# One transformer-like layer on one core: block transposes on VectorE, an accumulating residual and fewer loads for the weight sums

## The chip, the cores and the metric

The kernel runs on one core of a Trainium2 chip, in one launch. The metric is the device time of one execution in microseconds (us). The engines are PE (matrix multiply; PEld is its weight load), DVE (VectorE), ACT (ScalarE), POOL (GpSimd) and SP, which here issues nearly all DMAs. Each engine runs its own instructions strictly in the order in which the program put them; between engines, semaphores order them. All arithmetic and all data in DRAM are fp32.

## The reference

One layer over 2048 tokens of width 1024, with 256 memory tokens and a hidden width D_FF of 2816:

```python
u = rms_norm(h, g_mix_pre[l])
z = u @ w_in[l]
ya = swa_with_sinks(...)          # 64-wide heads, chunk-banded window
yh = hgrn2(...)                   # gated linear recurrence, 4 heads of 128
y = jnp.concatenate([ya, yh], axis=-1) @ w_out[l]
h = h + rms_norm(y, g_mix_post[l])
u = rms_norm(h, g_x_pre[l])
m = rms_norm(mem, g_mem[l])
y = cross_attention(u, m, wq_x[l], wk_x[l], wv_x[l], wo_x[l])
h = h + rms_norm(y, g_x_post[l])
u = rms_norm(h, g_ffn_pre[l])
y = (jax.nn.silu(u @ w_gate[l]) * (u @ w_up[l])) @ w_down[l]
h = h + rms_norm(y, g_ffn_post[l])
```

## The kernel before, in words

**How a large product is made.** Every fp32 factor is split into a high part (ACT copies it to the fp32r type, L994) and the rest (DVE subtracts, L997). A product is then three matmul passes: high by high, high by low, low by high (L1138, L1139, L1140 in `products`). On top of that, each block of 256 rows by 1024 columns is made by a Strassen-Winograd scheme of seven products instead of eight (`seven`, L1142). One of the seven is a **step**: four k-tiles by three passes, 12 matmuls of 128x128 stationary by 128x512 moving. The seven stationary operands S of a block are formed as it comes (`streamed`, L1072): two loads "sraw", some sums on DVE (L1113), and the splits. The seven moving operands T of a stage stay in SBUF over many blocks (`resident`, L1001). Three of them are plain quarters of the stage's matrix. The other four are sums of quarters, which are made ahead of the stage by `combined` (L1034): loads of quarters into tiles called "extra" (or "g"), a DVE operation of 128x1024 (L1041), and a store to a DRAM buffer (qk_s, vo_s, u_s, d_s0 to d_s2, out_s), from which `resident` later loads them as "row" (for out_s also as "z").

**The stages**, in order: the projections of w_in (to 200 us), the two mixing branches (to 600 us), the folding of cross-attention's four weight matrices into two (`fold_cross`, to 760 us), and then the list of `jobs` which `phases` (L1226) runs:

- mixed: concatenated branches times w_out, residual, two norms (763 to 930 us)
- scores: queries times the folded keys, softmax (to 1110 us)
- values: probabilities times the folded values, `value_block` (L1617) (to about 1270 us)
- FFN, first and second token half (to about 2080 us)
- three parts of the down projection (to 2536 us)

In the first three and in the down parts a block is two tiles of 128 tokens, n and n+1. There are 8 blocks to a stage, of 7 steps each.

**What sets the order.** `phases` is a Python generator that emits one step of PE work at a time. Between two steps it emits, for each block that has ended, one more piece of its follow-up work (the generators `after`, which "yield" between pieces: one yield is one step of delay), the S tiles that are needed two steps on (`upto(need[g + 2])`), and the loads and splits of the next T. So the place of a piece on DVE, ACT, POOL and SP is counted in steps. `queued` and `behind` hold work back until an instruction that was emitted before is reached.

**A block of values.** `out` brings the two result tiles into SBUF and ACT squares them (tiles "junk", L1513). The follow-up: `rstds` turns four sums of squares into two factors by three small POOL operations (L1524, L1526, L1528); DVE scales both tiles (L1637); the rows of the residual h1, loaded by SP into two more row tiles, are added by DVE (L1641); SP stores the sum to `out`; ACT squares again; `rstds` again; DVE scales again (L1650) and the result is u, the input of the FFN. `transposed` (L1391) turns each tile of u with 8 PE transposes into two PSUM banks (L1399) and two ACT copies (L1400), and SP stores it to `u_d`, which holds features by tokens. For n of 4 to 7, `token_sums` also makes the T sums of the FFN's first half there. The FFN reads T from `u_d`: columns 0 to 1023 for the first token half, the rest for the second.

**What else exists already.** `blocked` and `store_blocked` (L1403, L1410) transpose a tile on DVE in 32x32 blocks (L1407) and store it in four parts; the results of mixed and scores go that way, and `streamed` reads them with `blocked=True`. `add` (L1540) is a DMA from POOL's queue that adds DRAM rows to an SBUF tile; the last down part uses it.

Of the kernel before, what the change touches and what calls it, by code (L numbers as in the profile page):

```python
# [11 lines left out]
F32 = mybir.dt.float32  # L12
# [36 lines left out]
class Layer:  # L49
# [111 lines left out]
    def run(self):  # L161
# [14 lines left out]
        self.u_d = tc.dram_tile([KT, P, T], F32, name="u_d")  # L176
# [17 lines left out]
    def mix(self):  # L194
        tc, I = self.tc, self.I
        kw = dict(reuse_waits="tile")
        with contextlib.ExitStack() as left:
# [66 lines left out]
            with (  # L264
# [20 lines left out]
    def fold_cross(self):  # L285
# [57 lines left out]
        for h in range(4):  # L343
            banks = [[self.bank(k) for k in "sh"] for _ in range(2)]
            for i in range(2):
# [6 lines left out]
                self.split(raw, wh, wl, "A")  # L352
                for mt in range(2):
# [107 lines left out]
    def in_first(self):  # L461
# [84 lines left out]
        phases = self.phases([(lambda i, j, a, n: raw[i, j][:, a:a + n, :], 4, blocks, None, {})], T)  # L546
# [454 lines left out]
    def resident(self, get, nk, key, dst, keep, sums):  # L1001
# [32 lines left out]
    def combined(self, get, nk, dst):  # L1034
# [3 lines left out]
        for a, b in halves:  # L1038
# [4 lines left out]

            for x, y, key in (((0, 1), (0, 0), 5), ((1, 1), (0, 1), 7), (None, (0, 0), 6), (None, (1, 0), 4)):
# [181 lines left out]
    def phases(self, jobs, first, prologue=None):  # L1226
# [51 lines left out]
        def half(g, tile):  # L1278

            if current[0] is None:  # L1280
# [14 lines left out]
                current[:] = [(k, self.resident(fetch(n, tile), jobs[n][1], p, dst, keep[n], jobs[n][3] is not None)), 0]  # L1295
# [54 lines left out]
        for _, nk, bl, _, beside in jobs:  # L1350
# [69 lines left out]
    def w_out(self, t, i, j, k0, n):  # L1420
        for s in range(1 if i else 2):
            d = t if i else t[64 * s:64 * s + 64]
            r = 512 + k0 * P if i else 256 * s + 64 * k0
            p = P if i else 64
            self.load(d, self.I["w_out"][r:r + p * n, j * 512:(j + 1) * 512].rearrange("(k p) d -> p k d", p=p))

    def sums(self, name, src, nk, *tiles):
# [8 lines left out]
        return dst, lambda: self.combined(get, nk, dst)  # L1436
# [13 lines left out]
    def jobs(self):  # L1450
# [7 lines left out]
        def ffn_u(b):  # L1458
            return lambda t, i, j, k0, n: self.load(
                t, self.u_d[4 * i + k0:4 * i + k0 + n, :, b * TB + j * 512:b * TB + (j + 1) * 512]  # L1460
                .rearrange("k p t -> p k t"))
# [4 lines left out]
        def sums(name, src, nk, other=None):  # L1466
            return self.sums(name, src, nk, self.extra_tile, other or self.gain_tile)
# [10 lines left out]
        jobs = [(self.w_out, 4, kinds([self.mixed_block(n) for n in range(0, NT, 2)], 1), self.out_sums, {1: [qk_s[1]]}),  # L1478
# [325 lines left out]
```

## Time and profile before

| | us |
|---|---|
| median of 3 runs | 2538.45 (2537.29 to 2541.59) |
| the profiled execution | 2537.71 |
| its span in the profile | 2536.0 |

The span is what the trace covers; 1.7 us of the execution lie around it. The granted PE clock was 0.998 of full speed over the span. A row of the timeline gives start, duration, engine, line, operation, `out<-in`, the shapes, and in brackets the idle time of that engine just before and what ended it. A matmul of the main products has a duration of 0.39 us, but they overlap: one starts every 0.2275 us. A row of windows gives, for a stretch of time, the busy time and count of each engine, the granted clock, the mean busy share of the 16 DMA engines and their GB/s. Tile names are the program's with the numbers left out; `psm` is the PSUM of the main products, `pss` one for transposes and small products, `psh` one of the fold.

### The profile page before, as it was taken

The numbers are of one execution on the slowest core, as the hardware profiler recorded it, in microseconds if no ns is written. First come the engines' busy times: TensorE is split into PE (matmuls) and PEld (weight loads), VectorE is DVE, ScalarE is ACT, GpSimd is POOL, SyncE is SP. The second block draws the span as 40 slices with busy tenths as digits, with TensorE's granted clock in tenths as the row PEclk, the third lists the DMA queues.
The fourth block names the chain that finished last, engine by engine and source line by source line (L and its number), as shares of the span: only waits on it lengthen the run. The fifth ranks groups of instructions, "written<-read, shape, count | busy, mean of one in ns | idle before, by whom it ended". The sixth has DMA issues, their size and how long they took to land.

```text
span 2536.0 us, 34175 instructions
## 1 busy us (share of the span) xinstructions
PE 2495.5 (98%) x11942; PEld 2085.2 (82%) x11942; DVE 1795.1 (71%) x2863; ACT 1261.0 (50%) x2627; POOL 378.1 (15%) x540
## 2 busy tenths in 40 slices
PE   9999999999999999999999999999999999999998
PEld 8878888888997778878878888888888888888886
DVE  8885588986556889888876655576566557574766
ACT  5553466654565576566753333353333335443543
POOL 4331344321401112112100000000000000000022
PEclk9999999999999999999999999999999999999999
DMA  6455644673897997857954522254465334564776
GB/s 200 149 166 174 179 143 156 211 239 110 265 322 277 311 329 203 272 186 242 338 177 162 170 83 92 75 199 161 155 216 195 137 121 158 179 186 108 232 174 151
DMA packets 314445, 482.13 MB, mean 190 GB/s; under 512 B 22048, under 2 KB 194080, under 8 KB 314272
## 3 DMA queue, kind: packets, MB, share of 16 engines
q1 hardware_dynamic: 308224, 457.92, 54.2%
q0 software_dynamic: 6048, 22.02, 4.9%
q8 instruction: 94, 1.54, 0.2%
q14 instruction: 79, 0.65, 0.1%
HBM read 313.14 MB, written 166.72 MB: 189 GB/s over the span
## 4 chain that ended last, share of the span: by engine, by line
PE 78%; DVE 8%; DMA 7%; issue 3%; ACT 3%; POOL 1%; SPq 1%; DVEq 0%; POOLq 0%; ACTq 0%
PE psm L1140 21%; PE psm L1138 21%; PE psm L1139 21%; PE psg L158 2%; PE psg L157 2%; PE psg L156 2%; DVE T L997 1%; DVE S L997 1%; DMA qd<-z_d 1%; DVE sum L1113 1%; DVE row L1407 1%; DMA h1t_d<-row 0%; DMA y_d<-sg 0%; DMA qk_s<-extra 0%; ACT junk L1513 0%
## 5 line engine op out<-in xcount | busy, mean ns | idle before, releaser
L1138 PE MATMUL psm<-T,S 128*128 128x512 f32 x2680 | 1033.8, 390 | 14.1 <-ACT part L1153 7.8
L1139 PE MATMUL psm<-T,S 128*128 128x512 f32 x2680 | 1042.3, 390 | 1.2 <-DVE T L997 1.1
L1140 PE MATMUL psm<-T,S 128*128 128x512 f32 x2680 | 1029.7, 390 | 4.8 <-DVE S L997 4.8
L1138 PEld LDWEIGHTS psm<-T,S 128*128 128x128 f32 x2680 | 502.9, 188 | 126.9 <-ACT part L1153 12.9
L1140 PEld LDWEIGHTS psm<-T,S 128*128 128x128 f32 x2680 | 503.1, 188 | 111.9 <-DVE S L997 7.8
L1139 PEld LDWEIGHTS psm<-T,S 128*128 128x128 f32 x2680 | 503.2, 188 | 107.3 <-DVE T L997 4.1
L994 ACT ACTIVATE S<-sum 128x512 fp32r<-128x512 f32 (+1 forms) x370 | 223.9, 620 | 372.7 <-PE psm L1140 270.1
L997 DVE TENSOR_TENSOR S<-sraw,S 128x512 fp32r<-128x512 f32 (+1 forms) x315 | 210.9, 678 | 213.9 <-ACT S L994 211.0
L1153 ACT ACTIVATE part<-psm 128x512 f32<-128x512 f32 x285 | 168.7, 597 | 252.9 <-PE psm L1140 235.2
L997 DVE TENSOR_TENSOR S<-sum,S 128x512 fp32r<-128x512 f32 (+1 forms) x388 | 257.4, 673 | 41.8 <-ACT S L994 38.0
L994 ACT ACTIVATE S<-sraw 128x512 fp32r<-128x512 f32 (+1 forms) x300 | 184.5, 618 | 111.2 <-PE psm L1140 107.0
L1546 POOL DMA_DIRECT2D y_d<-row x16 | 14.0, 877 | 1077.0 <-DVE row L1728 1026.1
L997 DVE TENSOR_TENSOR T<-row,T 128x1024 fp32r<-128x1024 f32 (+1 forms) x112 | 130.9, 1183 | 29.1 <-ACT T L994 27.9
L156 PE MATMUL psg<-u,whi 128*128 128x512 f32 x320 | 127.9, 400 | 0.8 <-DVE z L725 0.8
L158 PE MATMUL psg<-u,wlo 128*128 128x512 f32 x320 | 127.4, 399 | 0.0
L157 PE MATMUL psg<-u,whi 128*128 128x512 f32 x320 | 127.2, 398 | 0.0
L1513 ACT ACTIVATE junk<-row 128x512 f32<-128x512 f32 x160 | 99.6, 624 | 48.3 <-DVE row L1535 27.4
L994 ACT ACTIVATE T<-row 128x1024 fp32r<-128x1024 f32 (+1 forms) x112 | 113.4, 1032 | 11.1 <-DMA row<-in_w_down_dram 3.8
L1679 DVE TENSOR_TENSOR row<-psm,part 128x512 f32<-128x512 f32 x66 | 43.7, 687 | 67.7 <-PE psm L1140 67.7
L997 DVE TENSOR_TENSOR wlo<-raw,whi 128x1024 fp32r<-128x1024 f32 x52 | 64.1, 1233 | 34.3 <-ACT whi L994 22.7
L1688 DVE TENSOR_TENSOR part<-psm,part 128x512 f32<-128x512 f32 x66 | 43.8, 687 | 59.8 <-PE psm L1140 59.6
L1728 DVE TENSOR_TENSOR row<-psm,part 128x512 f32<-128x512 f32 x72 | 49.1, 688 | 49.5 <-PE psm L1140 49.4
(354 smaller groups left out, 3557.6 us busy)
## 6 DMA issues: line engine op xcount, KB each, us to landing
sraw<-in_w_gate_dram SPq DMA_DIRECT2D x44, 512.0 KB, 3.7
sraw<-in_w_up_dram SPq DMA_DIRECT2D x44, 512.0 KB, 3.7
hid_d<-row SPq DMA_DIRECT2D x44, 512.0 KB, 2.7
sraw<-hid_d SPq DMA_DIRECT2D x32, 512.0 KB, 4.2
sraw<-in_w_in_dram SPq DMA_DIRECT2D x48, 256.0 KB, 3.8
z_d<-pair SPq DMA_DIRECT2D x20, 512.0 KB, 3.3
raw<-in_w_in_dram SPq DMA_DIRECT2D x20, 512.0 KB, 5.3
z_d<-z SPq DMA_DIRECT2D x20, 512.0 KB, 3.6
```

What stands on the lines that cost most here:

```text
L156: nc.tensor.matmul(ps, ah, bh, start=(i == 0), stop=False)
L157: nc.tensor.matmul(ps, ah, bl, start=False, stop=False)
L158: nc.tensor.matmul(ps, al, bh, start=False, stop=(i == n - 1))
L994: self.nc.scalar.activation(hi, raw, AF.Copy)
L997: self.nc.vector.tensor_tensor(lo, raw, f32(hi), ALU.subtract)
L1138: nc.tensor.matmul(ps, s[:, 0, k, :], t[:, 0, k, :], start=st, stop=False, **kw)
L1139: nc.tensor.matmul(ps, s[:, 0, k, :], t[:, 1, k, :], start=False, stop=False, **kw)
L1140: nc.tensor.matmul(ps, s[:, 1, k, :], t[:, 0, k, :], start=False, stop=sp, **kw)
L1153: nc.scalar.activation(t, ps, AF.Copy)
L1513: self.nc.scalar.activation(junk, a, AF.Square, scale=float(D) ** -0.5, accum_out=to)
L1688: nc.vector.tensor_tensor(c, a, c, ALU.add)
L1728: nc.vector.tensor_tensor(d, a, b, ALU.add)
```

## The change

1. **Values, second token half (n of 8 and more, 8 tiles).** u is not transposed on PE. DVE transposes it in 32x32 blocks, and four stores to a tile put it into a new buffer `ut_d`. T of the FFN's second half (and its sums u_s) is read from `ut_d`, and `resident` splits it with rearranged patterns (`bytoken`). `u_d` keeps the first half alone.
2. **The residual there.** The 8 SP loads of h1 rows and the 8 DVE additions become 8 accumulating DMAs from POOL's queue, issued right behind the first scaling, and one more yield follows.
3. **The sums.** `combined` gets a third tile and loads each quarter once: 4 loads for a half of the k-tiles in place of 6, each issued 4 yields ahead of its use in place of 3. It holds for qk_s, vo_s, u_s and the three d_s; out_s keeps the old way. There are as many DVE operations and stores as before.
4. **w_out** is laid out anew on the host, so that a load of it is one transfer with rows of 4 KB.
5. **`halved`.** The first S tiles of the mixed job are queued behind a split (on ACT) late in the fold.

```diff
+        self.u_d = tc.dram_tile([KT, P, TB], F32, name="u_d")
+        self.ut_d = tc.dram_tile([NPB, 2, P, 512], F32, name="ut_d")
...
                 with self.queued(self.folded):
                     next(phases)
+                with self.queued(self.halved):
+                    next(phases)
+                    next(phases)
...
                 self.split(raw, wh, wl, "A")
+                if j == 3:
+                    self.halved = self.traced(mybir.EngineType.Activation)
...
+            if bytoken:
+                v = t.rearrange("p n (a k c) -> p k (n a) c", **bytoken)
+                c = v.shape[-1]
+                self.split2(v, *(dst[:, e, :, a * P:b * P].rearrange("p k (m c) -> p k m c", c=c) for e in range(2)),
+                            "A")
+                return
...
+            if three:
+                x = get(0, 0, 1, a, b - a)
+                t = get(1, 1, 1, a, b - a)
+                for _ in range(4):
+                    yield
+                put(7, t, x, ALU.subtract)
+                o = get(2, 0, 0, a, b - a)
+                for _ in range(4):
+                    yield
+                put(5, x, o, ALU.subtract)
+                yield
+                put(6, o, t, ALU.add)
+                x = get(0, 1, 0, a, b - a)
+                for _ in range(5):
+                    yield
+                put(4, x, o, ALU.subtract)
+                for _ in range(2):
+                    yield
+                continue
...
     def w_out(self, t, i, j, k0, n):
-        for s in range(1 if i else 2):
-            d = t if i else t[64 * s:64 * s + 64]
-            r = 512 + k0 * P if i else 256 * s + 64 * k0
-            p = P if i else 64
-            self.load(d, self.I["w_out"][r:r + p * n, j * 512:(j + 1) * 512].rearrange("(k p) d -> p k d", p=p))
+        self.load(t, self.I["w_out"][i, j, k0 // n])
...
         def ffn_u(b):
+            if b:
+                return lambda t, i, j, n0, n: self.load(
+                    t, self.ut_d[4 * j + n0:4 * j + n0 + n, i].rearrange("n p c -> p n c"))
...
         def sums(name, src, nk, other=None):
-            return self.sums(name, src, nk, self.extra_tile, other or self.gain_tile)
+            return self.sums(name, src, nk, self.extra_tile, other or self.gain_tile, self.row_tile)
...
-            x = [self.rows_of(self.h1_d, n + i) for i in range(2)]
+            late = n < NPB
+            x = [self.rows_of(self.h1_d, n + i) for i in range(2 * late)]
             for i in range(2):
                 nc.vector.scalar_tensor_tensor(y[i], y[i], r[:, i:i + 1], self.g_x_post, ALU.mult, ALU.mult)
-            yield
-            yield
+                if not late:
+                    self.add(y[i], self.h1_d, n + i)
+            for _ in range(2 if late else 3):
+                yield
             for i in range(2):
-                nc.vector.tensor_tensor(y[i], y[i], x[i], ALU.add)
+                if late:
+                    nc.vector.tensor_tensor(y[i], y[i], x[i], ALU.add)
...
             for i in range(2):
+                if n >= NPB:
+                    self.store_blocked(self.ut_d[n - NPB + i], self.blocked(y[i], self.row_tile()))
+                    yield
+                    continue
                 u[i] = self.transposed(y[i], y[i])
                 self.store_transposed(self.u_d, n + i, u[i])
```

How it moves instructions is shown at three places. **PE, in the second half of values**, where tile n = 8 (row_12345 before) is transposed between two steps. Before:

```order
L1140 MATMUL psm_12842<-T_11470,S_12792 128x512
L1399 MATMUL pss_12758<-ident,row_12345 128x128 x4
L1399 MATMUL pss_12764<-ident,row_12345 128x128 x4
L1138 MATMUL psm_12673<-T_11317,S_12690 128x512
L1139 MATMUL psm_12673<-T_11317,S_12690 128x512
```

After (L1169 to L1171 are the same three passes under new line numbers):

```order
L1170 MATMUL psm_12789<-T_11441,S_12742 128x512
L1171 MATMUL psm_12789<-T_11441,S_12742 128x512
L1169 MATMUL psm_12634<-T_11288,S_12651 128x512
L1170 MATMUL psm_12634<-T_11288,S_12651 128x512
```

The eight transposes are gone and one step follows the other directly. It is so for all eight tiles.

**POOL, from the first norm of block n = 8 on** (its sums of squares are q_s_12344 before and q_s_12315 after). Before, the first norm of n = 8, its second norm (q_s_12482), and the first norm of n = 10 (q_s_12564), one after the other:

```order
L1528 TENSOR_TENSOR q_r_12480<-q_w_12478,mhalf 128x2
L1524 TENSOR_TENSOR q_v_12663<-q_s_12482 128x2
L1526 TENSOR_SCALAR q_w_12665<-q_v_12663 128x2
L1528 TENSOR_TENSOR q_r_12667<-q_w_12665,mhalf 128x2
L1524 TENSOR_TENSOR q_v_12696<-q_s_12564 128x2
L1526 TENSOR_SCALAR q_w_12698<-q_v_12696 128x2
L1528 TENSOR_TENSOR q_r_12700<-q_w_12698,mhalf 128x2
```

After (the second norm of n = 8 is q_s_12453, the first of n = 10 is q_s_12531; h_d in the two DMA rows stands for the buffer h1):

```order
L1558 TENSOR_TENSOR q_r_12451<-q_w_12449,mhalf 128x2
L1572 DMA row_12316<-h_d 128x1024
L1572 DMA row_12352<-h_d 128x1024
L1554 TENSOR_TENSOR q_v_12656<-q_s_12453 128x2
L1554 TENSOR_TENSOR q_v_12662<-q_s_12531 128x2
L1556 TENSOR_SCALAR q_w_12658<-q_v_12656 128x2
L1556 TENSOR_SCALAR q_w_12664<-q_v_12662 128x2
L1558 TENSOR_TENSOR q_r_12660<-q_w_12658,mhalf 128x2
L1558 TENSOR_TENSOR q_r_12666<-q_w_12664,mhalf 128x2
```

The two accumulating DMAs stand in POOL's queue, and the second norm of one block and the first norm of the next are interleaved, with the second norm's first operation ahead.

**DVE, at the end of the fold**, where the low parts of the mixed job's first S tiles stand. Before (`kv`, L317, is the low part of the memory's projected values, written in eight pieces, of which the row here is the last; `wlo` is the low part of a weight block of the fold, and the fold's matmuls wait for both):

```order
L997 TENSOR_TENSOR S_8321<-sraw_8317,S_8321 128x512
L997 TENSOR_TENSOR S_8324<-sraw_8317,S_8324 128x512
L997 TENSOR_TENSOR wlo_8162<-raw_8159,whi_8161 128x1024
L997 TENSOR_TENSOR S_8327<-sraw_8319,S_8327 128x512
L317 TENSOR_TENSOR kv_1055_7829<-psh_8080,kv_1055_7828 128x256
L997 TENSOR_TENSOR S_8330<-sraw_8319,S_8330 128x512
```

After:

```order
L1003 TENSOR_TENSOR wlo_8151<-raw_8148,whi_8150 128x1024
L321 TENSOR_TENSOR kv_1055_7818<-psh_8069,kv_1055_7817 128x256
L1003 TENSOR_TENSOR wlo_8169<-raw_8166,whi_8168 128x1024
L1003 TENSOR_TENSOR S_8310<-sraw_8306,S_8310 128x512
L1003 TENSOR_TENSOR S_8313<-sraw_8306,S_8313 128x512
L1003 TENSOR_TENSOR S_8316<-sraw_8308,S_8316 128x512
L1003 TENSOR_TENSOR S_8319<-sraw_8308,S_8319 128x512
```

The S rows, of which three stood ahead of the last kv row, now all stand behind it.

More of the change, by code (lines that the diff above doesn't have):

```diff
@@ L1294, in half @@
                 left[k] = 2
-                current[:] = [(k, self.resident(fetch(n, tile), jobs[n][1], p, dst, keep[n], jobs[n][3] is not None)), 0]
+                current[:] = [(k, self.resident(fetch(n, tile), jobs[n][1], p, dst, keep[n], jobs[n][3] is not None,
+                                                jobs[n][5])), 0]
             k, f = current[0]
@@ L1349, in phases @@
         fresh = False
-        for _, nk, bl, _, beside in jobs:
+        for _, nk, bl, _, beside, _ in jobs:
             for i, (kind, _, out, follow, addend) in enumerate(bl):
@@ L1477, in jobs @@
         d_s = [sums(f"d_s{c}", src, nk) for c, (src, _, nk) in enumerate(down)]
[L1478 to L1480 removed]
+        jobs = [(self.w_out, 4, kinds([self.mixed_block(n) for n in range(0, NT, 2)], 1), self.out_sums, {1: [qk_s[1]]}, None),
+                (qk, 4, kinds([self.score_block(n) for n in range(0, NT, 2)]), qk_s[0], {1: [vo_s[1]]}, None),
+                (vo, 4, kinds([self.value_block(n) for n in range(0, NT, 2)]), vo_s[0], {}, None)]
         for b in range(NB):
```

21 lines of the change are left out of this document (10 added, 11 removed).

## The prediction

> **What bounds the kernel now.** First the page's head, the chain of waits and the list of PE's waits, then the windows by stage.
>
> ```profile
> span 2536.0 us, 34175 instructions
> PE 2495.5 (98%) x11942; PEld 2085.2 (82%) x11942; DVE 1795.1 (71%) x2863; ACT 1261.0 (50%) x2627; POOL 378.1 (15%) x540
> PE 78%; DVE 8%; DMA 7%; issue 3%; ACT 3%; POOL 1%; SPq 1%; DVEq 0%; POOLq 0%; ACTq 0%
> PE psm L1138 <- ACT part L1153: 7.8, 10, 1.4
> PE psm L1140 <- DVE S L997: 4.8, 5, 1.6
> 800.00:930.00 130.00, 125.18 (x546) 101.77 (x545) 112.84 (x148) 80.17 (x186) 26.41 (x46) 1.00 0.96 317
> 1110.00:1310.00 200.00, 194.06 (x906) 158.32 (x906) 165.99 (x209) 128.78 (x275) 32.08 (x48) 1.00 0.75 254
> 1700.00:2080.00 380.00, 380.00 (x1678) 314.75 (x1677) 237.08 (x349) 139.58 (x243) 0.00 (x0) 1.00 0.45 157
> ```
>
> PE is busy for 98% of the span and 78% of the chain that ended last is PE's. Its waits are short, and the two longest entries sum to 12.6 us. The FFN's second half is PE alone: 380.00 us busy of 380, so nothing that only speeds loads or DVE can gain there. 1678 matmuls in 380 us make 0.2265 us for one, and a block of seven steps of 12 takes 84 x 0.2265 = 19.0 us. Two stages touched by the change have idle PE time, mixed (800 to 930, 4.8 us) and values with the switch to the FFN (1110 to 1310, 5.9 us). In both DVE is busy for over 80% (112.84 of 130, 165.99 of 200). So PE work that is taken away counts in full, provided that DVE, in whose queue S and T are made, doesn't end last in its place.
>
> **The PE transposes of the second half.** Removed are 64 transposes and 16 ACT copies.
>
> ```profile
> 1143.94 0.39 PE L1138 MATMUL psm<-T,S 128*128 128x512 f32 x1
> 1144.17 1.03 PE L1399 MATMUL pss<-ident,row 128*128 128x128 f32 x8
> 1144.96 0.47 PE L1139 MATMUL psm<-T,S 128*128 128x512 f32 x1
> 1145.28 0.39 PE L1140 MATMUL psm<-T,S 128*128 128x512 f32 x1
> 1249.79 0.87 PE pss L1399 x8
> L1399 PE MATMUL pss<-ident,row x128: 270/272/273, 1144.2 to 1301.3; 128*128 128x128 f32 x128
> L1400 ACT ACTIVATE row<-pss x32: 576/592/642, 1144.8 to 1301.7; 128x512 f32<-128x512 f32 x32
> ```
>
> Eight transposes of a tile start at 1144.17 and the next product at 1144.96: 0.79 us. The matmul behind that one starts 0.32 later in place of 0.23, which adds 0.09. So a tile holds PE up for 0.88 us, and the chain shows 0.87 for a tile of the second half. Eight tiles: 8 x 0.87 = **-7.0 us**, on the bounding engine, where PE is busy before and behind. ACT loses 16 x 0.592 = 9.5 us, off the chain.
>
> **What DVE gets for it.** Two block transposes to a tile are added, and the residual's addition goes.
>
> ```profile
> L1407 DVE STREAM_TRANSPOSE row<-row x64: 660/672/708, 804.9 to 1106.0; 128x512 f32<-128x512 f32 x64
> L1641 DVE TENSOR_TENSOR row<-row,row x16: 1210/1218/1221, 1122.7 to 1277.8; 128x1024 f32<-128x1024 f32 x16
> ```
>
> 16 x 0.672 = 10.8 us come and 8 x 1.218 = 9.7 go: +1.0 us over some 75 us, beside PE, taken as 0. If DVE has no room there, it is +1.0. [...]
>
> T of the FFN's second half is split with rearranged patterns. The nearest rows are S from plain rows in mixed and from blocked rows in scores:
>
> ```profile
> L994 ACT ACTIVATE S<-sraw 128x512 fp32r<-128x512 f32 x16 | 9.9, 625 | 4.7 <-PE psm L1140 4.7
> L994 ACT ACTIVATE S<-sraw 128x512 fp32r<-128x512 f32 x20 | 12.5, 624 | 8.0 <-PE psm L1140 8.0
> ```
>
> 625 against 624 ns: no price for the pattern. The loads and the 32 stores to `ut_d` carry the same bytes as before. Taken 0.
>
> **The switch from values to the FFN.** PE waits there for a T:
>
> ```profile
> 1283.92 0.50 PE L1139 MATMUL psm<-T,S 128*128 128x512 f32 x1 [0.35 <-DVE T L997]
> 1286.62 0.50 PE L1139 MATMUL psm<-T,S 128*128 128x512 f32 x1 [0.76 <-DVE T L997]
> ```
>
> T's low part is a subtraction behind ACT's copy. ACT gets lighter, but its squares of the last block now wait for an accumulating DMA. The bounds are -1.1 (both waits go) and +2.2 (as long again for each of two). Taken 0.
>
> **`halved`.** At the end of the fold PE waited for DVE:
>
> ```profile
> 743.34 0.68 DVE L997 TENSOR_TENSOR S<-sraw,S 128x512 fp32r<-128x512 f32 x1
> 743.95 0.42 DVE L317 TENSOR_TENSOR kv<-psh,kv 128x256 fp32r<-128x256 f32 x1
> 744.42 0.50 PE L358 MATMUL psh<-whi,kv 128*128 128x512 f32 x1 [0.82 <-DVE kv L317]
> 763.20 0.39 PE L1138 MATMUL psm<-T,S 128*128 128x512 f32 x1
> ```
>
> The kv row starts when the S row ahead of it ends, and PE waited 0.82 us for it. The S rows now stand behind kv: **-0.8 us**, bounds -0.8 and 0. They are late by a few operations of 0.7 to 1.2 us, but the product that reads them starts only at 763.20, almost 19 us on. That row also shows no wait for w_out's loads, so these count 0; the same bytes come in fewer transfers.
>
> **The sums from four loads.** DVE stops twice in mixed for them or near them:
>
> ```profile
> 812.24 1.22 DVE L1041 TENSOR_TENSOR extra<-extra,row 128x1024 f32<-128x1024 f32 x1 [1.99 <-DMA h1t_d<-row]
> 811.32 0.50 PE L1138 MATMUL psm<-T,S 128*128 128x512 f32 x1 [1.72 <-ACT S L994]
> 812.94 0.50 PE L1138 MATMUL psm<-T,S 128*128 128x512 f32 x1 [0.88 <-ACT part L1153]
> 870.36 1.23 DVE L1041 TENSOR_TENSOR extra<-extra,row 128x1024 f32<-128x1024 f32 x1 [1.03 <-DMA qk_s<-extra]
> 873.44 0.50 PE L1140 MATMUL psm<-T,S 128*128 128x512 f32 x1 [1.09 <-DVE S L997]
> ```
>
> The transfers have a mean share of 0.96 in this stage, so a load less is worth something. The bounds are 0 and -(1.72 + 0.88 + 1.09) = -3.7. The first two PE waits begin before DVE's operation at 812.24 and are for ACT, so they need not go. The third follows the DVE stop at 870.36 and has its size. Taken **-1.0 us**. The sums of the down parts lie in the FFN, where PE has no idle time to give back.
>
> **The accumulating residual.** It is a transfer that DVE started from POOL's queue, in place of a load that was issued early and an addition.
>
> ```profile
> L1542 POOL DMA_DIRECT2D row<-y_d x12: 875/882/1237, 2394.5 to 2493.9; - x12
> DMA to landing us min/median/max: 5.0/7.9/8.8
> L75 SPq DMA_DIRECT2D row<-h_d x18: 332/587/1183, 1100.6 to 2479.4; - x18
> DMA to landing us min/median/max: 2.6/5.8/10.6
> L1637 DVE SCALAR_TENSOR_TENSOR row<-row,q_r,g 128x1024 f32<-128x1024 f32 x16 | 19.8, 1281 | 2.0 <-POOL q_r L1528 2.0
> L1524 POOL TENSOR_TENSOR q_v<-q_s 128x2 f32<-128x2 f32 x15 | 7.7, 510 | 135.2 <-ACT junk L1513 135.2
> L1526 POOL TENSOR_SCALAR q_w<-q_v 128x2 f32<-128x2 f32 x15 | 7.7, 512 | 1.3
> L1528 POOL TENSOR_TENSOR q_r<-q_w,mhalf 128x2 f32<-128x2 f32 x16 | 16.3, 1021 | 1.3
> 1210.00:1230.00 20.00, 20.00 (x98) 16.78 (x97) 18.08 (x26) 13.12 (x31) 3.85 (x6) 1.00 1.06 342
> 2440.00:2460.00 20.00, 20.00 (x90) 16.57 (x89) 12.26 (x17) 9.36 (x20) 4.75 (x7) 1.00 0.75 158
> ```
>
> It makes a ring. On POOL the second norm of block n now starts ahead of the first norm of block n+2. That second norm waits for ACT's squares, these for the accumulated tile. And behind the first norm of n+2 DVE's scaling waits, with the S and T splits of the coming steps queued behind it on DVE; PE waits for those. One turn: two scalings 2 x 1.28 = 2.6, the second tile's issue 0.9, landing 7.9, its two squares 1.2 (about what two halves of a copy take, 0.62 each), and six POOL operations 4 x 0.51 + 2 x 1.02 = 4.1: 16.7 us against a block's 19.0. So 2.3 us are left, and landing may take 10.2 us. Each us above that comes three times, at the three blocks that follow another one of the second half. With 7.9 it costs 0. With 10.6, the slowest of SP's loads of such rows, 0.4 x 3 = 1.2. With twice 7.9, 5.6 x 3 = 16.8. The 12 rows of such DMAs come from a stage with DVE busy 12.26 of 20 and transfers at 0.75; in values it is 18.08 and 1.06. So I go near the 10.6 and take **+0.8 us**, bounds 0 and +16.8.
>
> **The reordering elsewhere** (the window branch near 440 to 600, fold, mixed) carries the same work; taken 0, bounds -3 and +3.
>
> **Sum.** -7.0 - 0.8 - 1.0 + 0.8 = -8.0. Against the profiled execution: 2536.0 - 8.0 = 2528.0 for the span, with 1.7 around it 2529.7. That execution lies 0.74 below the median of the runs, so the forecast is **2530.5 us**. Its own range, with 0 to -3.7 for the sums, 0 to 1.2 for the ring and 2 us for the reordering, is 2526 to 2534.
>
> **The rivals.** What counts as no change is 0.2%, 5.1 us.
>
> *A, the ring binds a little* (0.13). Landing takes half as long again as 7.9, 11.9 us: (11.9 - 10.2) x 3 = +5.1 in place of the 0.8, 2534.8, within 0.2%. For it: the 1.06 of transfers. Against it: the longest of twelve took 8.8.
>
> *B, the ring binds in full: slower* (0.14). Landing 15.8 us, or an issue on POOL that is held up as long: 16.8 - 0.8 = 16 above the forecast, 2546.5. The whole gain is gone from a landing of 10.2 + 8/3 = 12.9 us. For it: DVE is idle for only 2 of 20 us there, and SP's stores of the sum, which wait for the accumulate, stand ahead of loads of the next T. Against it: issues took 0.875 to 1.237 us beside a DVE that was busy 61%. [...] The twelve rows here show no issue held for longer than 0.4 us.
>
> *C, DVE becomes the bound in values* (0.09). DVE has 34 us of 200 idle, but in pieces; if S is made late by what PE saves, the first term is lost, +7.0 and +1.0 for DVE's own: 2538.5, no change. Against it: the longest waits of PE for DVE are 4.8 us in the whole run.
>
> *D, the waits go too* (0.08). -7.0 - 0.8 - 3.7 - 1.1 = -12.6: 2525.9.
>
> **How the numbers follow.** Forecast 0.56 and D 0.08 make faster 0.64; A and C make same 0.22; B is slower 0.14. The range 2524 to 2541 leaves out B and a little of D.
>
> **What would show it.** No PE transposes behind about 1210 us, and PE's busy time less by 6.4 to 7. The ring shows in ACT's squares waiting for the accumulating DMA, in its landing time against 10.2 us, and in DVE's scaling waiting for POOL. The sums show in PE's wait near 873, `halved` in that near 744, and the switch in the T waits near 1284. I am wrong if the landing is above 13 us, if PE's idle time between 1110 and 1310 grows by over 3 us, or if a stage that the edits don't touch moves by more than that.

## The result and the profile after

The change makes the kernel slower by 0.2%, which is about what the prediction counted as no change, but clear of the noise. Its median is 2543.64 us over 22 runs, against 2538.82 for the kernel before over 22 runs on the same chips; the ratio is 1.0020, with an interval of 1.0014 to 1.0025. One run of the change (9990.83 us) and one each of x2, x5 and x9 were slow ones, and all ratios leave them out. The prediction was 2530.5 us, faster.

The page of the changed kernel, its first lines and the chain:

```profile
span 2541.5 us, 34022 instructions
PE 2492.7 (98%) x11878; PEld 2081.6 (82%) x11878; DVE 1796.5 (71%) x2871; ACT 1252.9 (49%) x2611; POOL 377.7 (15%) x548
PE 80%; DVE 7%; DMA 5%; issue 3%; ACT 3%; POOL 1%; SPq 1%; DVEq 0%; POOLq 0%; ACTq 0%
```

The 64 transposes are gone from PE (11878 matmuls in place of 11942), yet its busy time falls by 2.8 us and not by 7. Where the time goes is read from the first and last start of lines that both kernels have. First the scalings of values and the first operation on a down block before, then the same two (L1668, L1766) after:

```profile
L1637 DVE SCALAR_TENSOR_TENSOR row<-row,q_r,g x16: 1275/1280/1287, 1120.3 to 1268.6; 128x1024 f32<-128x1024 f32 x16
L1728 DVE TENSOR_TENSOR row<-psm,part x72: 679/691/692, 2116.3 to 2523.6; 128x512 f32<-128x512 f32 x72
```

```profile
L1668 DVE SCALAR_TENSOR_TENSOR row<-row,q_r,g x16: 1277/1282/1286, 1113.3 to 1273.5; 128x1024 f32<-128x1024 f32 x16
L1766 DVE TENSOR_TENSOR row<-psm,part x72: 680/691/692, 2119.5 to 2528.7; 128x512 f32<-128x512 f32 x72
```

At the first scaling the changed kernel is 7.0 us ahead, at the last 4.9 us behind. So in these two traces values, where 7 us were to be gained, lose 11.9; one trace each places such a loss only to a few us. Some of it returns at the switch to the FFN (3.2 us behind at the down parts' start), and another 1.9 us go in the down parts, which no edit touches beyond their sums. The windows of the stage after the change:

```profile
1110.00:1310.00 200.00, 185.05 (x811) 149.89 (x811) 158.75 (x206) 117.89 (x254) 37.06 (x56) 0.97 0.82 250
1210.00:1230.00 20.00, 16.54 (x67) 13.18 (x66) 11.44 (x15) 8.33 (x20) 5.26 (x8) 0.91 0.96 319
1250.00:1270.00 20.00, 15.23 (x60) 12.11 (x59) 16.62 (x20) 12.96 (x25) 4.40 (x8) 0.85 1.01 313
```

PE is idle for 15.0 us in place of 5.9, and the granted clock is 0.97 in place of 1.00 over 200 us, which is an estimated 6 us more (0.03 of 200). The three longest waits of PE in the second half:

```profile
1218.94 0.50 PE L1171 MATMUL psm<-T,S 128*128 128x512 f32 x1 [3.46 <-DVE S L1003]
1265.95 0.79 PE L1169 MATMUL psm<-T,S 128*128 128x512 f32 x1 [4.77 <-ACT part L1184]
1287.66 0.62 PE L1169 MATMUL psm<-T,S 128*128 128x512 f32 x1 [1.93 <-ACT T L1000]
```

Behind the first stands DVE's queue, where the token sums (L1469) wait for the store of u of n = 7; behind the second ACT's queue, where the squares wait for the accumulating DMA:

```profile
1217.59 0.69 DVE L1469 TENSOR_TENSOR row<-row 128x512 f32<-128x512 f32 x1 [5.47 <-DMA u_d<-row]
```

```profile
1259.73 0.63 ACT L1543 ACTIVATE junk<-row 128x512 f32<-128x512 f32 x1 [3.34 <-DMA row<-h_d]
```

The store of u of n = 7 is late because SP issues it late. ACT's copies for it end at 1204.89, but on SP a store of the sum, which waits 2.5 us for the accumulating DMA, and two more issues stand ahead of it (these rows have start, duration, queue and DMA). It is issued 5.9 us after the copies and lands after 6.8. Before, it was issued as soon as the copies had ended, at 1211.77, and landed after 6.0. First the change, then before:

```profile
1207.97 0.38 SPq L78 DMA_DIRECT2D out_dram<-row  x1
1210.80 0.89 SPq L78 DMA_DIRECT2D u_d<-row  x1
```

```profile
1211.79 0.36 SPq L78 DMA_DIRECT2D u_d<-row  x1
```

So both long stalls lead back to a queue that stands at the landing of an accumulating DMA. The DMAs themselves landed as forecast; this is the line of the eight new ones:

```profile
DMA to landing us min/median/max: 5.4/8.5/10.1
```

### The profile page after: what moved, and what is told of

The parts are those of the page before. It is cut to its first block, busy times and chain, and to the rows that moved or that the text cites. A ratio compares the mean times of both kernels' runs of the same rounds, so it can differ in the third digit from the quotient of the medians.

```text
span 2541.5 us, 34022 instructions
## 1 busy us (share of the span) xinstructions
PE 2492.7 (98%) x11878; PEld 2081.6 (82%) x11878; DVE 1796.5 (71%) x2871; ACT 1252.9 (49%) x2611; POOL 377.7 (15%) x548
## 4 chain that ended last, share of the span: by engine, by line
PE 80%; DVE 7%; DMA 5%; issue 3%; ACT 3%; POOL 1%; SPq 1%; DVEq 0%; POOLq 0%; ACTq 0%
PE psm L1171 21%; PE psm L1169 21%; PE psm L1170 21%; PE psg L156 2%; PE psg L157 2%; PE psg L158 2%; DVE S L1003 1%; DVE T L1003 1%; DMA row<-h_d 1%; DMA pair<-in_x_dram 1%; ACT junk L1543 1%; DMA row<-u_s 1%; DMA ut_d<-row 1%; DVE sum L1144 1%; PE psh L157 0%
## 5 line engine op out<-in xcount | busy, mean ns | idle before, releaser
L1169 PE MATMUL psm<-T,S 128*128 128x512 f32 x2680 | 1036.3, 391 | 21.3 <-ACT part L1184 10.4
L1171 PE MATMUL psm<-T,S 128*128 128x512 f32 x2680 | 1032.4, 391 | 7.6 <-DVE S L1003 7.6
L1169 PEld LDWEIGHTS psm<-T,S 128*128 128x128 f32 x2680 | 504.6, 188 | 134.4 <-ACT part L1184 14.8
L1171 PEld LDWEIGHTS psm<-T,S 128*128 128x128 f32 x2680 | 504.9, 188 | 116.3 <-DVE S L1003 11.4
L1000 ACT ACTIVATE T<-row 128x1024 fp32r<-128x1024 f32 (+1 forms) x112 | 113.3, 1029 | 11.8 <-DMA row<-d_s 4.8
L1766 DVE TENSOR_TENSOR row<-psm,part 128x512 f32<-128x512 f32 x72 | 49.2, 688 | 49.4 <-PE psm L1171 49.3
L832 ACT ACTIVATE S<-S,w_mn 128x256 f32<-128x256 f32 (+1 forms) x128 | 63.1, 496 | 42.5 <-DVE w_mn L828 42.0
```

The lines of the kernel that those rows point to most:

```text
L832: nc.scalar.activation(s[:, r, o:], s[:, r, o:], AF.Exp, bias=mn[:, i:i + 1], scale=-1.0, accum_out=den[:, i:i + 1])
L1000: self.nc.scalar.activation(hi, raw, AF.Copy)
L1169: nc.tensor.matmul(ps, s[:, 0, k, :], t[:, 0, k, :], start=st, stop=False, **kw)
L1171: nc.tensor.matmul(ps, s[:, 1, k, :], t[:, 0, k, :], start=False, stop=sp, **kw)
L1766: nc.vector.tensor_tensor(d, a, b, ALU.add)
```

## The experiments

Each kernel is compared with the kernel before on the same chip. The table gives the ratio to it; one thousandth is 2.5 us.

| kernel | ratio, interval |
|---|---|
| the change | 1.0020 (1.0014 to 1.0025) |
| x1 the change, residual loaded | 0.9995 (0.9985 to 1.0005) |
| x2 before, residual accumulated | 1.0016 (1.0004 to 1.0028) |
| x3 the change, sums of six loads | 1.0031 (1.0022 to 1.0041) |
| x4 before, w_out repacked | 0.9988 (0.9978 to 0.9998) |
| x5 the change without halved | 1.0016 (1.0007 to 1.0024) |
| x7 x1, block stores from POOL | 1.0009 (0.9999 to 1.0018) |
| x8 before with sums, w_out, halved | 0.9987 (0.9978 to 0.9996) |
| x9 before, block transposes | 1.0016 (1.0006 to 1.0026) |
| x10 x1, residual added by POOL | 1.0033 (1.0020 to 1.0045) |
| x11 before, 16 more DVE transposes | 1.0019 (1.0008 to 1.0029) |
| x12 before, 32 more stores | 0.9995 (0.9986 to 1.0004) |
| x13 x2, waits later | 1.0018 (1.0009 to 1.0028) |
| x14 x2, sum stored by POOL | 1.0042 (1.0029 to 1.0056) |
| x15 x1 without the additions | 0.9979 (0.9970 to 0.9988) |
| x16 before with sums, w_out | 0.9979 (0.9969 to 0.9989) |
| x17 before, 8 more accumulating DMAs | 1.0018 (1.0009 to 1.0027) |
| x18 before, 8 more plain DMAs from POOL | 1.0005 (0.9996 to 1.0014) |

### Which part costs

x1 undoes the second part, x2 and x4 do one part alone, x3 undoes the third.

```diff
 x1, in value_block of the change
-            x = [self.rows_of(self.h1_d, n + i) for i in range(2 * late)]
+            x = [self.rows_of(self.h1_d, n + i) for i in range(2)]
-                if not late:
-                    self.add(y[i], self.h1_d, n + i)
...
+                nc.vector.tensor_tensor(y[i], y[i], x[i], ALU.add)
```

> The change with its second part undone: the residual rows of the second token half are again loaded by SP and added by DVE, and the third yield goes. Theory R (the accumulating DMA is what costs): in the profile of the change SP's stores of the sum wait for it, and ACT's squares wait for it (3.3 us once), and two of PE's stalls, 3.46 and 4.77 us, follow. Without it both stalls go with the low clock behind them: about 2530 us (2527 to 2533), PE idle time between 1110 and 1310 us under 7 us. Rival T (the block transposes on DVE, or the four stores and the T loads from the new buffer, are what costs): 2541 to 2545 us, stalls of PE of 3 us and more remain.

```diff
 x2, in value_block of the kernel before: the same lines the other way round
+                if not late:
+                    self.add(y[i], self.h1_d, n + i)
```

> The kernel before with the second part alone: the residual of the second half by accumulating DMA from POOL's queue, PE transposes kept. Theory R: slower than before by 8 to 17 us, 2547 to 2555 us, with PE stalls of 3 us and more behind 1195 us. Rival T: within 3 us of before, 2536 to 2541 us.

```diff
 x3, in jobs of the change
-            return self.sums(name, src, nk, self.extra_tile, other or self.gain_tile, self.row_tile)
+            return self.sums(name, src, nk, self.extra_tile, other or self.gain_tile)
```

> The change without its third part: each half of the sums takes six loads again. As the prediction has it the four loads give 1.0 us: 2544.6 us. Rival: the row tile that they hold for longer takes room from the follow-up work, and without it the time is 2 us shorter or more, 2541.5 us or less.

```diff
 x4, in w_out of the kernel before, with the host's repacking
+        self.load(t, self.I["w_out"][i, j, k0 // n])
```

> The kernel before with the fourth part alone: w_out in one load of 4 KB rows. In the trace of the change PE reaches the end of the mixing branches 4.3 us earlier than before, and nothing but this part lies there (22 loads less in SP's queue between 440 and 725 us). Theory W (the loads, by the order that they change): 2534 to 2536 us, PE at the end of the branches 2 to 4.3 us earlier. Rival: the 4.3 us are not this part's, time 2537.5 to 2540 us as the prediction had it at 0.

x2 is 1.6 thousandths slower than before (2544.1 us, between the times of its two theories), and x1 is 2.5 faster than the change: the accumulating residual costs 4 to 6 us against loads and additions on DVE. But x1 only comes back to the kernel before (2538.3 us), where theory R had 2530, so there is a second loss. x3 puts the sums at 1.1 thousandths within the change, about 2.8 us, where 1.0 us was forecast; the intervals of the two ratios overlap. x4 is faster by 1.2 thousandths, near theory W's time. But the 4.3 us that W read from two traces do not bear it out. The first wait in mixed, a gap of 1.72 us for ACT's S, ends at 811.32 in the profile of before and at 806.66 in that of x14, with the same instructions up to there. So one trace against another can't place a gain of 4 us in that part, and where w_out's 3 us arise is left open.

x5 and x9 go on with single parts, x8 leaves the first two out, and x7 tries the first explanation for the second loss.

```diff
 x5, at the start of mixed in the change
-                with self.queued(self.halved):
-                    next(phases)
-                    next(phases)
 x7, in store_blocked, for the eight tiles of values, on top of x1
+            if pool:
+                self.nc.gpsimd.dma_start(dst[:, :, a * P:(a + 1) * P].rearrange("h (b i) s -> i (h b) s", b=4),
+                                         t[a * 32:(a + 1) * 32, :].rearrange("i (g s) -> i g s", g=8))
+                continue
 x8: the kernel before with the diffs of combined, sums, w_out and halved
 x9: the kernel before with the diffs of resident, ffn_u and transposition
+                if n >= NPB:
+                    self.store_blocked(self.ut_d[n - NPB + i], self.blocked(y[i], self.row_tile()))
```

> The change without its fifth part (the first S tiles of mixed are not queued behind the fold's split). As the prediction has it: 0.8 us slower than the change, 2543.5 to 2545 us, and PE's wait for kv near 740 us back. Rival: the late S tiles cost more at the start of mixed than the wait was worth, and the time is 1 us or more below the change.

> The change with the residual loaded again (as in x1_residual_loaded, 2538.3 us) and the 32 stores of the block-transposed tiles issued from POOL's queue in place of SP's. Theory S: in x1's trace the four stores of a tile hold SP's queue for 2.3 to 2.8 us in place of 0.4 for the one store before, the loads of T's sums behind them come late, ACT waits for one 2.54 us, a copy of a result behind it is late, PE stands for 2.71 us and its clock is halved for 10 us behind that. With the stores off SP's queue these go: 2530 to 2534 us, clock not halved between 1190 and 1310 us. Rival D: the loads are late for the transfers' sake, or DVE is what is short, and the time stays at 2537 to 2540 us.

> The kernel before with the third, fourth and fifth part (sums, w_out, halved), PE transposes and loaded residuals kept. If the parts add up as the runs so far have them (w_out alone -3.0, sums -4.0 within the change, halved -0.8 by the prediction): 2531 us. Rival: the sums' gain in the change was one of its own stalls that moved, and here they give 1 us: 2534 us or more.

> The kernel before with the block transposes alone (first part; residual loaded, six loads, old w_out, no halved). Theory S: the 7 us of PE transposes are given back by stalls at the end of values and the halved clock behind them: 2540 to 2547 us, no faster than before. Rival: the first part is worth its 7 us alone and only clashes with another part: 2530 to 2533 us.

x9 finds the second loss: the block transposes alone, with the additions still on DVE, make the kernel before 1.6 thousandths slower, 4 us, though they take 7 us of work from PE. x8 is faster by 1.3 (2535.9 us, as its rival had it, where the sum of the parts was 2531). x5 can't be told from the change (intervals 1.0007 to 1.0024 and 1.0014 to 1.0025), so `halved` did not give 0.8 us that show. x7 refutes theory S, which had 2530 to 2534 us: with the stores off SP's queue it takes 2540.9, and PE still stalls for 2.79 us up to 1269.43. In its trace that wait is for DVE.

### Why the block transposes cost

The view that answers it is the windows of 10 us at the end of values. Before (1260 to 1280), then x1 (1250 to 1270):

```profile
1260.00:1270.00 10.00, 10.00 (x49) 8.36 (x49) 10.00 (x11) 9.85 (x18) 2.38 (x3) 1.00 1.02 384
1270.00:1280.00 10.00, 10.00 (x48) 8.07 (x47) 10.00 (x12) 4.59 (x8) 0.00 (x0) 1.00 0.97 341
```

```profile
1250.00:1260.00 10.00, 9.33 (x41) 7.42 (x40) 10.00 (x14) 8.51 (x18) 4.08 (x6) 1.00 1.00 320
1260.00:1270.00 10.00, 6.46 (x21) 4.42 (x20) 10.00 (x12) 4.88 (x7) 0.00 (x0) 0.81 1.02 361
```

Already before, DVE (the third engine of a row, behind PE and PEld) is busy without a break from 1260 to 1280 us: the follow-up of the last blocks and the low parts of the FFN's T fall together there. PE transposed two tiles meanwhile, at 1266.17 and 1271.39. With block transposes DVE gets 1.34 us more for each tile (2 x 0.672), and PE, which now has less to do, waits. Four kernels test this:

```diff
 x10, on top of x1
-                nc.vector.tensor_tensor(y[i], y[i], x[i], ALU.add)
+                (nc.vector if n < NPB else nc.gpsimd).tensor_tensor(y[i], y[i], x[i], ALU.add)
 x11, in the kernel before
+                if n >= NPB:
+                    self.blocked(y[i], self.row_tile())
 x12, in the kernel before
+                if n >= NPB:
+                    self.store_blocked(self.ut_d[n - NPB + i], y[i])
 x15, on top of x1
-                nc.vector.tensor_tensor(y[i], y[i], x[i], ALU.add)
+                if n < NPB:
+                    nc.vector.tensor_tensor(y[i], y[i], x[i], ALU.add)
```

> x1_residual_loaded (2538.3 us), but the eight additions of the residual run on POOL in place of DVE. Theory D: in x1 DVE is busy for 10.00 of 10 us in 1250 to 1260 and in 1260 to 1270 us, and PE for 6.46 in the second; DVE has become the bound at the end of values, where it also makes the low parts of the FFN's T. Taking 9.7 us from DVE, some 5 of them in that stretch, gives back 4 to 8 us with the halved clock: 2530 to 2534.5 us. Rival S (SP's queue and the transfers of T's sums): DVE idles for what it saves, time 2537 to 2540 us.

> The kernel before with 16 block transposes more on DVE in the second half of values, whose result is stored nowhere; PE transposes and all transfers stay. Theory D: DVE has no room at the end of values (10.00 of 10 us in 1260 to 1280 us before), 16 x 0.67 = 10.8 us of work cost 3 to 8 us: 2541 to 2546 us. Rival S: hidden, 2537 to 2540 us.

> The kernel before with 32 stores more from SP's queue in the second half of values (each tile of u a second time, in four stores of 32 rows, to a buffer that nothing reads). Theory D: 2537 to 2540 us, the queue has room. Rival S: SP's queue is held some 2.5 us a tile and T's loads come late, 2541 us or more.

> x1_residual_loaded (2538.3 us) without the eight additions of the residual of the second token half, which are left out of the computation; the loads stay. Nothing is put on another engine for it. Theory D: DVE is 9.7 us lighter, about 5 of them at the end of values, PE's stalls there shrink and the clock stays whole: 2530 to 2534.5 us. Rival: DVE is full there because its work comes late (loads of T's sums), not because it is too much: 2536.5 to 2540 us.

x11 and x12 separate the theories: 10.8 us of DVE work that nobody reads cost 1.9 thousandths, 4.8 us, and 32 further stores cost nothing that shows. x15 is the other side: 9.7 us less on DVE bring x1's 0.9995 to 0.9979, 2532.7 us. The windows of x11 and of x15:

```profile
1270.00:1280.00 10.00, 8.28 (x39) 5.90 (x38) 9.99 (x12) 9.33 (x13) 0.63 (x1) 1.00 0.84 278
1280.00:1290.00 10.00, 9.64 (x47) 7.74 (x46) 10.00 (x14) 4.71 (x8) 0.00 (x0) 1.00 0.98 334
```

```profile
1250.00:1260.00 10.00, 10.00 (x46) 8.28 (x45) 10.00 (x13) 8.08 (x15) 4.39 (x5) 1.00 1.03 310
1260.00:1270.00 10.00, 8.63 (x37) 6.53 (x36) 9.10 (x11) 5.72 (x8) 1.36 (x2) 1.00 1.01 388
```

In x11 PE keeps its transposes and still loses 1.7 us in 1270 to 1280 with DVE full; over 1110 to 1310 it is idle for 8.9 us, against 5.9 before. In x15 PE is busy for 8.63 of the 10 us in which x1 had 6.46. x10 missed: an addition takes POOL 2.77 to 4.46 us in place of DVE's 1.22, the second norm comes later by that, and DVE stays full until 1290 us. It says nothing for or against DVE as the bound.

x15 comes near the forecast, but not by the forecast's way. It has all parts of the change but the accumulating DMA, whose rows are loaded as before, and DVE carries what the prediction gave it there, 10.8 us more and 9.7 less. x8 has the same other parts and PE's transposes. Between 1110 and 1310 us DVE is busy for 163.4 us in both, yet x15 is only 0.8 thousandths faster (0.9979 against 0.9987), 2 us with room for nothing to some 5, where 7.0 were forecast. DVE is busy for 38.2 of the 40 us from 1250 to 1290 in x15. So the time that PE spent on transposes was in large part time in which DVE would have kept it waiting. x16 below, with PE's transposes kept, is as fast as x15.

### Why the accumulating residual costs

x13 lets three more steps pass before anything waits for the DMA; x14 issues the store of the sum from POOL.

```diff
 x13, on top of x2
-            for _ in range(2 if late else 3):
+            for _ in range(2 if late else 6):
 x14, on top of x2
-                self.store((self.out if n < NT - 2 else self.h2_d)[(n + i) * P:(n + i + 1) * P, :], y[i])
+                (nc.sync if late else nc.gpsimd).dma_start(
+                    (self.out if n < NT - 2 else self.h2_d)[(n + i) * P:(n + i + 1) * P, :], y[i])
```

> x2_residual_added_alone (2544.1 us against 2539.0 of before) with three more yields between the accumulating DMA and what waits for it (SP's store of the sum and ACT's squares). Theory Q (what costs in x2 is that SP's and ACT's queues stand at these two waits): the waits are over when they are reached, 2534 to 2539.5 us. Rival B (the transfer itself, or its issue on POOL, disturbs): 2542 us or more.

> x2_residual_added_alone (2544.1 us against 2539.0 of before) with the stores of the sum, which wait for the accumulating DMA, issued from POOL's queue for the second half. Theory Q2: in x2 SP's store of the sum of n = 8 waits for that DMA, the store of u of n = 7 stands behind it (1215.96 in place of 1211.79 us), DVE's token sums wait 4.73 us for that one, PE stands for 2.80 us and its clock is halved for 6.8 us. With the stores off SP's queue the wait of the token sums falls back to about 1 us and the stall goes: 2536 to 2540.5 us. Rival B (landing, issue on POOL, or the squares' wait): 2542 us or more.

x13 stays slow (1.0018). In its trace no square of ACT waits for the DMA any more between 1190 and 1300 us, and the cost stays, so ACT's wait is not needed for it. But the first store of the sum still stands ahead of the store of u of n = 7, so x13 says nothing of SP's queue. x14 takes the store of the sum off SP, and DVE's token sums still wait for the store of u, even longer than in x2 (4.73 us):

```profile
1220.72 0.69 DVE L1441 TENSOR_TENSOR row<-row 128x512 f32<-128x512 f32 x1 [6.26 <-DMA u_d<-row]
```

As a whole x14 is slower still (1.0042); its traced run is the fastest of its five, 2540.8 us against 2547 to 2550. The store of u can be late in SP's queue, behind ACT's copies, or by its landing. It stood in the queue for 4.8 us in x2 and 3.9 in x14, where before it stood 0.0, and it landed after 7.2 and 9.7, where before it took 6.0. So in x2 it is mostly the queue, and x14, where a store of T's sums and a load stand ahead of it without the store of the sum, does not clear the queue. The landing is the other part. The DMA rows for 1195 to 1295 us show what bears on it. Each row of a queue gives packets, MB and the share of the 16 engines' time; an issue row ends with the median time to landing. Before, then x2:

```profile
q1 hardware_dynamic: 25675, 31.15, 89.8%
u_d<-row SPq DMA_DIRECT2D x8, 512.0 KB, 6.5
```

```profile
q1 hardware_dynamic: 24354, 26.84, 77.1%
q0 software_dynamic: 1152, 4.19, 23.0%
u_d<-row SPq DMA_DIRECT2D x8, 512.0 KB, 8.6
```

The eight accumulating transfers (q0) hold all 16 engines for 23 of 100 us. At the rate of the other queue (31.15 MB in 89.8%) their 4.19 MB would take an estimated 12.1. The two queues together fill 100% of the stretch, and the eight stores of u land 2 us later in the median. The last two kernels take this by itself:

```diff
 x17 and x18, in the kernel before, behind the addition; the result is read by nothing
+                if n >= NPB:
+                    self.add(x[i], self.h1_d, n + i)                                      (x17)
+                    nc.gpsimd.dma_start(x[i], self.h1_d[(n + i) * P:(n + i + 1) * P, :])  (x18)
```

> The kernel before, with eight accumulating DMAs more from POOL's queue in the second half of values, into the residual tiles after they have been added; nothing reads the result, so nothing waits for it but the tiles' next use. Theory X (the accumulating transfer itself: in x2 between 1195 and 1295 us its 4.19 MB took 23.0% of the 16 DMA engines' time, 23.0 us, where at the 31.15 MB in 89.8% of before they would take 12.1; in a stretch that is 90% full the other landings come late, u_d<-row in 8.6 in place of 6.5 us): 2541 to 2546 us. Rival Q (the waits of SP's store and of ACT's squares for it): 2537 to 2540 us.

> As x17_extra_accumulating, with plain loads of the same rows from POOL's queue in place of the accumulating DMAs. Theory X: 12 us of transfers in place of 23, partly in the room that is left: 2537.5 to 2541 us, below x17. Rival Q: as x17, both without effect. If it is as slow as x17 above 2541 us, it is any 4.19 MB more, or POOL's issues, and not the accumulation.

x17 costs 1.8 thousandths, 4.5 us, with nothing that waits for the result; x18 costs 0.5 or nothing (the intervals overlap a little). In x17 the store of u of n = 7 is issued on time but lands after 11.8 us, in x18 after 9.5. The rows of q0, first x17's, then x18's with its other queue and its stores of u:

```profile
q0 software_dynamic: 1143, 4.19, 21.4%
```

```profile
q1 hardware_dynamic: 25248, 31.17, 87.9%
q0 software_dynamic: 1152, 4.19, 10.7%
u_d<-row SPq DMA_DIRECT2D x8, 512.0 KB, 9.2
```

The same bytes took twice the engine time when they were accumulated (21.4% against 10.7% of 100 us), and by x17 the transfers alone can cost as much as x2 does. They do not settle what x2 pays for. x2 drops eight loads, so on balance it adds an estimated 11 us of engine time (23.0 less 12.1), about as much as x18, and x18, with the stretch 99% full and the stores of u landing later still, costs 0.5 or nothing. x2 also has SP's new order, which x17 and x18 have not. How its 4 us divide between the transfers and SP's queue is open. The added yield was not tried by itself.

In the change the price is higher. x15 has neither the accumulating DMA nor the additions, and the change is 4.1 thousandths slower than it, 10.4 us. That is more than twice x17's 4.5 us, and the two long stalls of the change go through SP's wait of 2.5 us and ACT's of 3.34. That these waits make up the difference fits, but no run took them out of the change with the transfers kept.

### A version that beats both

x16 keeps the third and fourth part.

```diff
 x16: the kernel before with the diffs of combined, sums and w_out
```

> The kernel before with the third and fourth part alone (four-load sums, w_out), without halved. If halved gives 0.8 us as predicted, 0.8 us above x8_without_first_two: 2536.7 us, or 0.9990 of before. If halved costs about 1 us, as the run of the change without it hints (0.9996 of the change), 0.9983 of before or less.

It is 0.9979 of before (0.9969 to 0.9989), 2533.5 us against 2538.2, and faster than both kernels. Against x4 the sums give 0.9 thousandths, 2.3 us, and against x8 `halved` seems to cost 0.8, but in both cases the intervals overlap.

## Why the prediction was wrong

**The steps that failed** are two terms of the sum. The first is the -7.0 for PE's transposes, which was to count in full "provided that DVE [...] doesn't end last in its place". DVE's +1.0 us, 10.8 of new work against 9.7 taken away, was set against the mean of the stage (165.99 busy of 200) and "taken as 0". The work lands in the last blocks, where the windows of before show 10.00 of 10. With DVE loaded just as forecast, the part gave 2 us of the 7 (x15 against x8); with the additions left on DVE it costs 4 (x9).

The second is the +0.8 for the accumulating residual. It costs 4 us by itself (x2), 6.3 within the change against loads and additions (x1), and 10.4 against x15. The ring that was worked out for it did not bind: landing had a median of 8.5 us and at most 10.1, within the 10.2 allowed, and DVE's scaling waited for POOL 1.1 us in four times (before 2.0 in six). But the ring followed the landing on one way alone, through POOL to DVE's scaling. Two queues that stand at the same landing were put at nothing: SP's, where the store of u of n = 7 came 5.9 us late, and ACT's, which stood for 3.34 us (the prediction named ACT's squares for the last block alone, and took them as 0). Left out as well was the transfer's price to the others: the row of 1.06 in 1210 to 1230 us was read as a risk for this DMA's landing alone.

**The size of the miss.** Taken from before to x8, x15 and the change, the first term gave 5 us less than forecast and the second cost 9.6 more. The other three parts gave 3.3 us (x8) in place of 1.8. Together these are the 13 us between forecast and result; each of the three has some 3 us of noise.

**Rival C** was the first mechanism, with 0.09. It was set aside because of "4.8 us in the whole run"; the row gives this as the sum of five waits, of which the longest took 1.6, so PE's waits for DVE were shorter still than the text has it. By x9, where stalls appear once PE's transposes are gone (2.17 us up to 1270.90), they were short since PE had its transposes to do. And the rival was priced at no change, without the stalls' own cost in clock (0.57 from 1270 to 1280 us in x9). **Rival B** had the sign and nearly the time. Its landing of 15.8 us did not come, but it named one true way: that SP's stores of the sum wait for the accumulate, with other DMAs behind them.

**The smaller terms.** The sums came out at 2.3 us (x16 against x4) or 2.8 (x3), where -1.0 was taken; the noise leaves room for that. w_out was taken as 0 with the same bytes in fewer transfers and gave 3.0 (x4, interval 0.5 to 5.6). `halved`'s 0.8 was not seen; PE's wait for kv is gone from the list of waits, but no gain can be told. **Added up** from single parts, in thousandths: 1.6 (x9) + 1.6 (x2) - 1.2 (x4) - 0.9 (x16 to x4) + 0.8 (x8 to x16) = 1.9, against 2.0 measured. With about one thousandth of noise on each, the agreement is partly luck: x2's DMA takes the additions from DVE, which x15 shows to be worth 1.6 when block transposes are there, so its own price must be higher in the change.

**The signs named beforehand:** PE's transposes end at 1203.8, as said. ACT's squares did wait for the accumulating DMA. PE's busy time fell by 2.8 in place of 6.4 to 7; behind the stalls, where the clock was 0.50 to 0.60, matmuls lasted 0.63 us in place of 0.39, and that time counts as busy. PE's idle time between 1110 and 1310 grew by 9.0, three times the bound that was named for being wrong.

## What to carry to other kernels

Cost moved work against the engine's busy time in windows of about one block at the place where it lands, above all where two stages overlap; a stage mean can hide a stretch that is full, as DVE's 165.99 of 200 us hid 20.00 of 20. Work that looks like the bounding engine's burden may be what it does while it waits for another: of the 7 us of transposes x15 gave 2 against x8. Before a result is handed to a DMA, list every queue that stands at its landing, and what stands behind in each. Where the DMA share is near 1, price a transfer by the engine time of its kind and not by its bytes alone (here 21.4% against 10.7% of 100 us for the same 4.19 MB).

## What the runs showed of the hardware

The eight accumulating DMAs from POOL into SBUF took twice the DMA engine time of eight plain ones from the same queue: 21.4% (x17) to 23.8% (the change) of 100 us against 10.7% (x18) for the same 4.19 MB.

Two stalls of PE in the change cost more than their length. Windows cut at them, with the clock third from the end:

```profile
1215.00:1219.00 4.00, 0.54 (x4) 0.11 (x2) 1.41 (x3) 3.91 (x10) 0.85 (x2) 1.00 1.11 368
1219.00:1222.50 3.50, 3.50 (x10) 2.72 (x11) 2.48 (x4) 0.00 (x0) 3.01 (x4) 0.59 1.04 337
1261.00:1266.00 5.00, 0.23 (x2) 0.06 (x1) 4.04 (x6) 5.00 (x13) 0.50 (x2) 0.80 0.95 282
1266.00:1272.00 6.00, 6.00 (x17) 4.71 (x18) 3.58 (x4) 3.79 (x6) 2.11 (x5) 0.60 1.01 379
1272.00:1276.00 4.00, 4.00 (x18) 3.00 (x17) 4.00 (x6) 2.65 (x5) 1.64 (x2) 1.00 1.08 404
```

Behind the stall of 3.46 us PE ran at a granted clock of 0.59 for 3.5 us, with ten matmuls begun where the next 3.5 us hold 16; behind the one of 4.77 us it ran at 0.60 for 6. Behind the 1.93 us at 1287.66 the matmuls that follow take 0.63 us in place of 0.39, at a clock of 0.50 from 1288 to 1290. The gap of 1.72 us in mixed, with one of 0.88 close behind it, was followed by a clock of 0.55 (x11) and 0.51 (x12) from 811 to 818 us and by one of 1.00 in the profile of before, with the same instructions up to there. What decides whether the clock falls behind such a gap is not shown by these runs.
